# Context transposes by the PSUM bank, a bank for each value block, and the second layer's tables ahead of its weights

## The chip, the cores and the metric

The kernel runs on one core of one Trainium2 chip. Time is the device time of that core in microseconds, from the first to the last instruction of one execution. It was 2702.51 us before the change, the median of three runs (2702.22 to 2703.63).

## What is computed

Two layers over 512 latent tokens and 256 context tokens, 1024 channels each, in float32. Cut to what matters here:

```python
for l in range(2):
    h_lat = rmsnorm(x, g_norm1[l]) * (1 + sc1) + sh1          # 512 tokens
    h_ctx = rmsnorm(ctx, g_norm1[l]) * (1 + csc1) + csh1      # 256 tokens
    p_lat = h_lat @ w_in[l]       # queries, keys, values, two convolutions, gates
    p_ctx = h_ctx @ w_in[l]       # in the last layer keys and values alone
    q, k  = rope(rmsnorm(heads(...)))        # per head; the context's without rope
    x   = x + gt1 * (merge of attention and convolutions) @ w_o[l]
    x   = x + gt2 * relu(modulated norm of x @ w_mlp_in[l])**2 @ w_mlp_out[l]
    # ctx goes the same way in the first layer
return rmsnorm(x, g_final)
```

Latent queries attend to latent and context keys together, context queries to context keys alone.

## The kernel before

**Numbers.** Every float32 operand of a matmul is split into a high and a low half, and one product is three matmuls (`mm3`: L163 high by high, L164 high by low, L165 low by high). Weights come by SP's DMA queue into a ring of four raw buffers `wraw` (L126 for query and key columns, L128 for others); ACT casts the high half (L134, `whi`), and DVE or POOL subtracts for the low one (L136, `wlo`).

**Tiles.** Tokens stand in six blocks of 128, four latent and two of context (in the trace of the second layer's start these are the last two that the first layer's MLP makes). Activations go into the matmuls transposed, channels on partitions, in eight tiles (`k` or `j` from 0 to 7, called columns below). PSUM has two pools that matter: `pa` tiles of two banks, `pb` tiles of one bank.

**From the residual stream to a projection** (`modulate`). When a block's MLP output is complete in PSUM, DVE multiplies it by the gate (L1116, `gt`) and adds it to the residual (L1117), ACT sums its squares (L1093), POOL makes the root (L378, L379), DVE scales the block (L1095). Then PE transposes column by column (L428). For the 512 latent tokens one column fills a bank, for the 256 context tokens half of one. Each column is evicted twice: ACT writes the high half (L433, modulated by scale and shift), and a second copy is made from the same PSUM, by DVE for even columns (L438) and by ACT for odd ones (L436); DVE subtracts for the low half (L439). Before the change the two columns of a context bank are transposed one after the other, each in its own step.

**Queries, keys, values.** The combined projection of queries and keys runs for the latent tokens, then for context. Four `pb` tiles are copied out by ACT (L500) and DVE (L502), squared on ACT (L512), turned by the rotary tables on DVE (L522, L525; the tables are multiplied by the gains at L472), scaled on POOL (L555, L563, L565) and transposed (L534). The values (`v_heads`) take two token blocks into the two halves of one `pb` tile, and each half is split on its own (ACT L156, DVE L159). Scores, softmax and the products with the values follow (L665 to L693).

**What sets the order.** The code is a set of generators that are stepped beside one another; a scheduler then fixes the order of the instructions of each engine, by its own estimate of times, and that order is the program. `next_in` is the step that puts the second layer's first loads, table products, modulation and projection beside the end of the first layer's MLP. `tc.issue_after(x)` keeps an instruction behind `x`. Each engine works through its own list in order, and SP's list is that of the loads.

## Time and profile before

| | |
|---|---|
| median of three runs | 2702.51 us |
| the profiled execution's own time | 2700.5 us |
| its span | 2698.7 us |
| granted TensorE clock, mean | 0.999 |
| PE busy | 2672.6 us (99%) |
| DVE / ACT / POOL busy | 1624.6 / 873.9 / 693.3 us |

Spans and shares are those of one execution. A row of a timeline gives start, duration, engine, line, operation, names out<-in, sizes, and in brackets the idle time of the engine ahead of it with what ended it. Matmuls overlap: the distance from one start to the next is what one costs, 0.23 us for 512 columns, while the duration of one is longer. A wait of PE is counted only where PE itself was idle.

### The profile page before, as it was taken

What the parts mean: (1) busy time and instruction counts of PE and PEld (TensorE: products, weight loads), DVE (VectorE), ACT (ScalarE), POOL (GpSimd) and SP (SyncE); (2) the same over time, 40 slices, a digit from 0 to 9 for tenths busy, and PEclk for the clock granted to TensorE, in tenths of its full rate; (3) what the DMA queues carried; (4) which work ended last, traced back from release to release, by engine and by line L of the source; (5) the groups of instructions that cost most, each with busy time, mean ns of one, the idle gap of its engine ahead of it and who ended that gap; (6) DMA issues with size and microseconds to landing.
All of it is one profiled execution on the core that took longest, in us unless ns stands there. A gap on an engine that the chain in (4) does not pass through costs nothing.

```text
span 2698.7 us, 36188 instructions
## 1 busy us (share of the span) xinstructions
PE 2672.6 (99%) x14571; PEld 2300.5 (85%) x14571; DVE 1624.6 (60%) x2098; ACT 873.9 (32%) x1426; POOL 693.3 (26%) x593
## 2 busy tenths in 40 slices
PE   8999999999999999999999999999999999999998
PEld 5899888888888888888888888998888888888887
DVE  5656837897764335585445356657578645644545
ACT  4556222122212323412121235563223233422223
POOL 1433432243221220201010103335445212111102
PEclk9999999999999999999999999999999999999999
DMA  7211324432275243344334232114333634432332
GB/s 255 64 35 58 98 77 141 133 107 66 82 228 157 63 144 94 97 159 153 110 104 146 79 110 87 55 60 122 120 114 102 181 112 144 132 95 94 110 101 94
DMA packets 341983, 302.50 MB, mean 112 GB/s; under 512 B 10577, under 2 KB 288385, under 8 KB 341817
## 3 DMA queue, kind: packets, MB, share of 16 engines
q1 hardware_dynamic: 340400, 298.81, 35.8%
q8 instruction: 114, 1.87, 0.3%
q10 hardware_dynamic: 1416, 1.39, 0.2%
q14 instruction: 53, 0.43, 0.0%
HBM read 274.96 MB, written 25.20 MB: 111 GB/s over the span
## 4 chain that ended last, share of the span: by engine, by line
PE 96%; DVE 2%; DMA 1%; ACT 1%; issue 0%; POOL 0%; SPq 0%; POOLq 0%; ACTq 0%; DVEq 0%
PE pa L163 21%; PE pa L165 21%; PE pa L164 21%; PE pb L163 9%; PE pb L165 8%; PE pb L164 8%; PE pb L676 2%; PE pb L690 1%; PE pb L693 1%; PE pb L691 1%; DVE tx L522 1%; PE pa L428 0%; DVE wlo L136 0%; PE pb L918 0%; PE pb L784 0%
## 5 line engine op out<-in xcount | busy, mean ns | idle before, releaser
L163 PE MATMUL pa<-ta,whi 128*128 128x512 f32 (+1 forms) x2896 | 1023.9, 354 | 0.0
L164 PE MATMUL pa<-ta,wlo 128*128 128x512 f32 (+1 forms) x2896 | 1020.1, 352 | 0.0
L165 PE MATMUL pa<-ta,whi 128*128 128x512 f32 (+1 forms) x2896 | 1019.6, 352 | 0.0
L134 ACT CAST whi<-wraw 128x1024 fp32r<-128x1024 f32 x360 | 377.8, 1051 | 1036.5 <-PE pa L165 404.3
L163 PEld LDWEIGHTS pa<-ta,whi 128*128 128x128 f32 x2896 | 547.9, 189 | 78.5 <-issue 2.5
L165 PEld LDWEIGHTS pa<-ta,whi 128*128 128x128 f32 x2896 | 547.4, 189 | 75.0 <-DVE ta L439 0.2
L164 PEld LDWEIGHTS pa<-ta,wlo 128*128 128x128 f32 x2896 | 548.0, 189 | 73.4
L163 PE MATMUL pb<-whi,ta 128*128 128x512 f32 (+1 forms) x1200 | 435.2, 363 | 3.5 <-ACT ta L433 1.9
L165 PE MATMUL pb<-wlo,ta 128*128 128x512 f32 (+1 forms) x1200 | 432.5, 361 | 1.5 <-DVE wlo L136 1.5
L164 PE MATMUL pb<-whi,ta 128*128 128x512 f32 (+1 forms) x1200 | 432.9, 361 | 0.0
L760 DVE SCALAR_TENSOR_TENSOR pv<-tx,cols,pv 128x783 f32<-128x783 f32 (+1 forms) x448 | 400.9, 895 | 12.6
L136 DVE TENSOR_TENSOR wlo<-wraw,whi 128x1024 fp32r<-128x1024 f32 x248 | 322.7, 1304 | 89.3 <-ACT whi L134 83.5
L136 POOL TENSOR_TENSOR wlo<-wraw,whi 128x1024 fp32r<-128x1024 f32 x112 | 270.2, 2414 | 360.2 <-ACT whi L134 308.0
L163 PEld LDWEIGHTS pb<-whi,ta 128*128 128x128 f32 x1200 | 226.8, 189 | 41.7 <-ACT ta L433 2.6
L982 POOL TENSOR_TENSOR ta<-ta 128x768 fp32r<-128x768 f32 (+1 forms) x64 | 105.0, 1641 | 600.2 <-DVE ta L981 593.7
L165 PEld LDWEIGHTS pb<-wlo,ta 128*128 128x128 f32 x1200 | 226.7, 189 | 35.2 <-DVE wlo L136 1.7
L164 PEld LDWEIGHTS pb<-whi,ta 128*128 128x128 f32 x1200 | 227.0, 189 | 34.7 <-issue 0.8
L315 DVE SCALAR_TENSOR_TENSOR tx<-wraw,cs,tx 128x1024 f32<-128x1024 f32 x112 | 157.9, 1424 | 49.0 <-DMA wraw<-in_w_mod 44.1
L979 DVE TENSOR_SCALAR ta<-pa 128x512 f32<-128x512 f32 (+1 forms) x63 | 51.8, 822 | 192.5 <-PE pa L165 181.9
L1116 DVE TENSOR_TENSOR ta<-pb,gt 128x512 f32<-128x512 f32 x100 | 68.8, 688 | 160.0 <-PE pb L165 159.9
L803 ACT ACTIVATE ta<-pa 128x768 f32<-128x768 f32 (+1 forms) x52 | 36.6, 705 | 223.8 <-PE pa L165 215.1
L159 POOL TENSOR_TENSOR ta<-tx,ta 128x768 fp32r<-128x768 f32 (+1 forms) x32 | 52.6, 1643 | 156.2 <-ACT ta L156 151.7
(188 smaller groups left out, 2352.0 us busy)
## 6 DMA issues: line engine op xcount, KB each, us to landing
wraw<-in_w_in SPq DMA_DIRECT2D x144, 512.0 KB
wraw<-in_w_mod SPq DMA_DIRECT2D x80, 512.0 KB
wraw<-in_w_mlp_out SPq DMA_DIRECT2D x72, 512.0 KB
wraw<-in_w_mlp_in SPq DMA_DIRECT2D x64, 512.0 KB
wraw<-in_w_o SPq DMA_DIRECT2D x24, 512.0 KB
tx<-spill SPq DMA_DIRECT2D x24, 384.0 KB
ta<-in_w_mod SPq DMA_DIRECT2D x32, 256.0 KB
wraw<-in_w_attn_out SPq DMA_DIRECT2D x16, 512.0 KB
```

What stands on the lines that cost most here:

```text
L134: nc.scalar.copy(hi, raw)
L136: self.last_lo = self.lo_engine.tensor_tensor(lo, raw, hi.bitcast(F32), op=ALU.subtract)
L159: (eng or nc.gpsimd).tensor_tensor(lo, src, hi.bitcast(F32), op=ALU.subtract)
L163: nc.tensor.matmul(ps, ah, bh, start=start, stop=False)
L164: nc.tensor.matmul(ps, al, bh, start=False, stop=False)
L165: self.last_pe = nc.tensor.matmul(ps, ah, bl, start=False, stop=stop)
L315: nc.vector.scalar_tensor_tensor(acc[b], raw, c, acc[b], op0=ALU.mult, op1=ALU.add)
L676: nc.tensor.transpose(pt[:, b * 256 + q * P:b * 256 + (q + 1) * P], probs[n, part][q][:, o], self.ident)
L760: nc.vector.scalar_tensor_tensor((v if t == K_CF - 1 else pv)[:, 0:n], u[:, t:t + n], c["cf"](t, k), (v if t == 1 else pv)[:, 0:n], op0=AL ...
L979: nc.vector.tensor_scalar(out=v[:, 0:n], in0=ps[:, 0:n], scalar1=0.0, scalar2=None, op0=ALU.max)
L982: nc.gpsimd.tensor_tensor(lo[:, 0:n], v[:, 0:n], hi[:, 0:n].bitcast(F32), op=ALU.subtract)
L1116: nc.vector.tensor_tensor(t, ps, gt[:, o], op=ALU.mult)
```

## The change

Five things are done.
- `modulate`: for a wide tile with context tokens, both columns of a bank are transposed in the even column's step, four transposes in a row.
- `v_heads`: each of the six value blocks has a `pb` tile of its own. The weights of the values are requested ahead of the late keys (`w_v`).
- Keys and queries: in the first layer the context's pair, in the second layer the second latent pair too, are made after these requests (`late`).
- `next_in`: the rotary tables of the second layer are requested first, its query and key weights behind the last of them; the products of tables and gains move from ahead of the projection to its middle (`CTX_FROM` is 4).
- Gate rows and the last norm's gains are requested behind the last weight load so far. In `scores`, the context's two matmul groups run one behind the other before the first softmax.

```diff
--- before.py
+++ after.py
@@ -123,9 +123,9 @@
         raw = self.W("wraw", N_RAW, shape)
         if isinstance(src, list):
             for k, part in enumerate(src):
-                nc.sync.dma_start(out=raw[:, k].rearrange("p (s c) -> p s c", s=2), in_=part)
+                self.last_load = nc.sync.dma_start(out=raw[:, k].rearrange("p (s c) -> p s c", s=2), in_=part)
         else:
-            nc.sync.dma_start(out=raw, in_=src)
+            self.last_load = nc.sync.dma_start(out=raw, in_=src)
         return raw
 
     def halves(self, raw, shape):
@@ -366,7 +366,8 @@
         got = []
         for b in range(nb):
             t = self.small.tile([P, D], F32, name="gt", tag="gt", bufs=2)
-            self.nc.sync.dma_start(out=t, in_=self.gates[l, r][b:b + 1, :].broadcast_to([P, D]))
+            with self.tc.issue_after(self.last_load.ins):
+                self.nc.sync.dma_start(out=t, in_=self.gates[l, r][b:b + 1, :].broadcast_to([P, D]))
             got.append(t)
         return got
 
@@ -420,12 +421,17 @@
             if wide and not pre and j % (1024 // n) == 0:
                 pa = self.PA()
             at = j % (1024 // n) * n
+            bank = 512 // n if wide else 1
             if pre:
                 ps = pre.pop(0)
             else:
+
                 ps = pa[:, at:at + n] if wide else self.PB()
-                for q, xn in enumerate(xns):
-                    nc.tensor.transpose(ps[:, q * P:(q + 1) * P], xn[:, j * P:(j + 1) * P], self.ident)
+                to = pa[:, at:] if wide else ps
+                for u in range(bank if j % bank == 0 else 0):
+                    for q, xn in enumerate(xns):
+                        nc.tensor.transpose(to[:, u * n + q * P:u * n + (q + 1) * P],
+                                            xn[:, (j + u) * P:(j + u + 1) * P], self.ident)
             a = self.scale[l][:, which, b, j:j + 1]
             s0 = 0 if which == 0 else 24
             sh = self.mc[l][:, b, s0 + j:s0 + j + 1]
@@ -461,7 +467,7 @@
             gains.append(g)
         for g in gains:
             rope = self.X(D)
-            nc.sync.dma_start(out=rope, in_=i["rope"])
+            self.last_rope = nc.sync.dma_start(out=rope, in_=i["rope"])
             ropes.append(rope)
         self.tables = gains, ropes
 
@@ -576,7 +582,9 @@
         kt = self.new_pairs(2)
         new_queries(0)
         gains, ropes = self.tables
-        for p, (tk, tq) in enumerate(pairs):
+        pairs = list(enumerate(pairs))
+        late = pairs[2 if l == 0 else 1:]
+        for p, (tk, tq) in pairs[:len(pairs) - len(late)]:
             key(tk, p)
             query(0, tq, p)
         pa = self.PA()
@@ -588,22 +596,23 @@
                 c = slice((NB_L + b) * P, (NB_L + b + 1) * P)
                 self.mm3(ps[b][:, o], hs[k][0][:, c], hs[k][1][:, c], ws[k][0][:, o], ws[k][1][:, o],
                          k == 0, k == KT - 1)
-        tk, tq = self.qk_out(ps, full)
-        key(tk, 2)
-        if full:
-            query(0, tq, 2)
+        late.append((2, self.qk_out(ps, full)))
+        w_v = self.w_rows(w, 0, OFF_V, 256)
+        for p, (tk, tq) in late:
+            key(tk, p)
+            if tq is not None:
+                query(0, tq, p)
         vt = self.new_pairs(2)
 
         def v_heads():
-            ws = self.w_rows(w, 0, OFF_V, 256)
+            ws = w_v
             for p in range(3):
-                ps = self.PB()
                 for b in range(2):
-                    blk = 2 * p + b
-                    self.gemm_tm(ps[:, b * 256:(b + 1) * 256], ws, hs, blk)
+                    blk, ps = 2 * p + b, self.PB()
+                    self.gemm_tm(ps[:, 0:256], ws, hs, blk)
                     hi, lo = vt[blk // 3]
                     o = slice((blk % 3) * 256, (blk % 3 + 1) * 256)
-                    self.split(ps[:, b * 256:(b + 1) * 256], hi[:, o], lo[:, o], eng=nc.vector)
+                    self.split(ps[:, 0:256], hi[:, o], lo[:, o], eng=nc.vector)
                 yield True
 
         spill = [self.spill([P, T]) for _ in range(8)]
@@ -648,7 +657,9 @@
                     p = self.A() if part else self.X(T)
                 else:
                     sv = s[:, q * TC:(q + 1) * TC]
-                    self.mm3(sv, qh[:, o], ql[:, o], kh[:, TL:T], kl[:, TL:T], True, True)
+                    for u in range(2 if q == 0 else 0):
+                        c = slice((blk + u) * P, (blk + u + 1) * P)
+                        self.mm3(s[:, u * TC:(u + 1) * TC], qh[:, c], ql[:, c], kh[:, TL:T], kl[:, TL:T], True, True)
                     p = self.X(TC)
                 a = 4 * q
                 nc.vector.tensor_reduce(out=m[:, a:a + 1], in_=sv, axis=AX.X, op=ALU.max)
@@ -1017,7 +1028,8 @@
             self.bg.append(nxt)
         else:
             gf = self.small.tile([P, D], F32, name="gt", tag="gt", bufs=2)
-            nc.sync.dma_start(out=gf, in_=i["g_final"][None, :].broadcast_to([P, D]))
+            with self.tc.issue_after(self.last_load.ins):
+                nc.sync.dma_start(out=gf, in_=i["g_final"][None, :].broadcast_to([P, D]))
             self.g_final = gf
             self.ys = {}
         self.lo_engine = nc.vector
@@ -1213,15 +1225,18 @@
     def next_in(self, ws):
 
         l = DEPTH - 1
-        raws = [self.w_qk(self.i["w_in"][l], u) for u in range(KT // 2)]
         self.rotary_in(l)
+        with self.tc.issue_after(self.last_rope.ins):
+            raws = [self.w_qk(self.i["w_in"][l], u) for u in range(KT // 2)]
         for raw in raws:
             ws += self.qk_halves(raw)
-        self.rotary()
         ctx = self.ctx_in(l)
         for k in range(KT):
             for _ in range(4 if k == 0 else 1):
                 next(self.lat, None)
+            if k == CTX_FROM:
+                with self.tc.issue_after(self.last_dve.ins):
+                    self.rotary()
             for _ in range(CTX_STEP if k >= CTX_FROM else 0):
                 next(ctx, None)
             yield True
```

Line numbers shift: after the change the transposes are L433 (before L428), ACT's evictions L439 and L442 (L433, L436), DVE's L444 and L445 (L438, L439), the copies L506 and L508 (L500, L502), the rotary products L528 and L531 (L522, L525), the tables' product L478 (L472), and the residual chain L1105, L1107, L1128, L1129 (L1093, L1095, L1116, L1117).

Three places of the new order. The first is PE at the start of the second layer. Before, the end of the MLP's last block, four latent transposes (column 6), and the projection:

```order
L164 MATMUL pb<-whi,ta 128x512
L165 MATMUL pb<-wlo,ta 128x512
L428 MATMUL pa<-ident,tx 128x128 [waits PE_49,Activation_49]
L428 MATMUL pa<-ident,tx 128x128 x3
L163 MATMUL pb<-whi,ta 128x512 [waits Activation_49]
L164 MATMUL pb<-whi,ta 128x512
L165 MATMUL pb<-wlo,ta 128x512 [waits DVE_49]
L163 MATMUL pb<-whi,ta 128x512
```

After, from the latent columns 6 and 7 on, with the context's twelve transposes behind them:

```order
L433 MATMUL pa<-ident,tx 128x128 [waits PE_49,Activation_49]
L433 MATMUL pa<-ident,tx 128x128 x3
L433 MATMUL pa<-ident,tx 128x128 [waits DVE_49]
L433 MATMUL pa<-ident,tx 128x128 x3
L433 MATMUL pa<-ident,tx 128x128 [waits PE_49,Activation_49]
L433 MATMUL pa<-ident,tx 128x128 [waits DVE_49]
L433 MATMUL pa<-ident,tx 128x128 x2
L433 MATMUL pa<-ident,tx 128x128 [waits PE_49,Activation_49]
L433 MATMUL pa<-ident,tx 128x128 x3
L433 MATMUL pa<-ident,tx 128x128 [waits DVE_49,Activation_49]
L433 MATMUL pa<-ident,tx 128x128 x3
L163 MATMUL pb<-whi,ta 128x512 [waits Activation_49]
```

Twenty transposes stand together now. In the order, the wait for DVE ahead of the context's second transpose is for the last context block's norm (L1107), the last wait for DVE and ACT is for both evictions of the first context bank, and the matmul's wait is for the cast of its weights on ACT.

The second is ACT at the same place, with `pa_13757` and `pa_13811` (before) and `pa_13814` (after) latent tiles, `pa_13930` and `pa_13979` context tiles. Before, the cast `whi_13861` of the projection's first weights and what follows it:

```order
L134 CAST whi_13861<-wraw_13841 128x1024 [waits DMAHW5_49,DMAHW4_49,PE_49]
L433 ACTIVATE ta_13609<-pa_13757,mc1_149,scale1_151 128x512 [waits DVE_49,PE_49]
L436 ACTIVATE ta_13771<-pa_13757,mc1_149,scale1_151 128x512
L134 CAST whi_13865<-wraw_13844 128x1024 [waits DMAHW7_49,DMAHW6_49,PE_49]
L134 CAST whi_13869<-wraw_13847 128x1024 [waits DMAHW1_49,DMAHW0_49,PE_49]
L134 CAST whi_13873<-wraw_13850 128x1024 [waits DMAHW3_49,DMAHW2_49,PE_49]
L433 ACTIVATE ta_13611<-pa_13811,mc1_149,scale1_151 128x512 [waits PE_49]
L1093 ACTIVATE pa_13829,st_13830<-tx_9676 128x1024 [waits DVE_49,Activation_49]
```

After, from the squares of the last context block to the first of these casts, `whi_13864`:

```order
L1105 ACTIVATE pa_13832,st_13833<-tx_9679 128x1024 [waits DVE_49,Activation_49]
L439 ACTIVATE ta_13616<-pa_13814,mc1_149,scale1_151 128x512 [waits DVE_49,PE_49]
L442 ACTIVATE ta_13828<-pa_13814,mc1_149,scale1_151 128x512
L439 ACTIVATE ta_13602<-pa_13930,mc1_149,scale1_151 128x256 [waits PE_49]
L439 ACTIVATE ta_13610<-pa_13979,mc1_149,scale1_151 128x256 [waits PE_49]
L439 ACTIVATE ta_13604<-pa_13930,mc1_149,scale1_151 128x256 [waits DVE_49]
L442 ACTIVATE ta_13940<-pa_13930,mc1_149,scale1_151 128x256
L439 ACTIVATE ta_13606<-pa_13930,mc1_149,scale1_151 128x256 [waits PE_49]
L439 ACTIVATE ta_13608<-pa_13930,mc1_149,scale1_151 128x256 [waits DVE_49]
L442 ACTIVATE ta_13964<-pa_13930,mc1_149,scale1_151 128x256
L134 CAST whi_13864<-wraw_13852 128x1024 [waits DMAHW6_49,DMAHW5_49]
```

The first cast moved from ahead of the last context block's squares to behind the evictions of context columns 0 to 4.

The third is DVE in the first layer, where `pa_590` holds context columns 0 to 3 and `ta_720` (after: `ta_722`) is the copy of column 2. Before, from the last copy of the projection's results on:

```order
L502 COPY tx_640<-pb_304 128x256 [waits Activation_49]
L522 TENSOR_TENSOR tx_660<-tx_633,tx_438 128x512 [waits DVE_49]
L438 TENSOR_SCALAR ta_720<-pa_590,scale0_150,mc0_148 128x256 [waits Activation_49]
L522 TENSOR_TENSOR tx_654<-tx_633,tx_438 128x512 [waits Activation_49]
L522 TENSOR_TENSOR tx_678<-tx_634,tx_440 128x512 [waits DVE_49]
```

After:

```order
L508 COPY tx_640<-pb_304 128x256 [waits Activation_49]
L528 TENSOR_TENSOR tx_660<-tx_633,tx_438 128x512 [waits DVE_49]
L528 TENSOR_TENSOR tx_654<-tx_633,tx_438 128x512 [waits Activation_49]
L528 TENSOR_TENSOR tx_678<-tx_634,tx_440 128x512 [waits DVE_49]
L531 TENSOR_TENSOR tx_633<-tx_660,tx_654 128x512 [waits DVE_49]
L528 TENSOR_TENSOR tx_672<-tx_634,tx_440 128x512 [waits Activation_49]
L528 TENSOR_TENSOR tx_691<-tx_639,tx_438 128x512 [waits DVE_49]
L531 TENSOR_TENSOR tx_634<-tx_678,tx_672 128x512 [waits DVE_49]
L444 TENSOR_SCALAR ta_722<-pa_590,scale0_150,mc0_148 128x256 [waits PE_49]
```

The eviction moved from behind one rotary product to behind seven. On ACT, column 3's eviction stands behind sixteen squares there, and in the order the last four of these wait for the seventh product.

## Rows read from the trace of the kernel before

**Rows 1.** Page: busy us and share of engines; a group: busy, mean, idle time.

```profile
PE 2672.6 (99%) x14571; PEld 2300.5 (85%) x14571; DVE 1624.6 (60%) x2098; ACT 873.9 (32%) x1426; POOL 693.3 (26%) x593
...
L1116 DVE TENSOR_TENSOR ta<-pb,gt 128x512 f32<-128x512 f32 x100 | 68.8, 688 | 160.0 <-PE pb L165 159.9
```

**Rows 2.** Waits of PE over the span: us in total, times, longest us.

```profile
PE pa L428 <- DVE ta L438: 1.8, 2, 1.0
PE pb L690 <- DVE tx L159: 1.8, 2, 0.9
PE pb L165 <- DVE wlo L136: 1.5, 1, 1.5
PE pb L534 <- DVE ta L159: 1.1, 2, 0.6
PE pb L163 <- DVE ta L159: 0.9, 1, 0.9
```

**Rows 3.** Timeline of PE at the end of the MLP: start us, duration us.

```profile
1615.88 0.39 PE L165 MATMUL pb<-wlo,ta 128*128 128x512 f32 x1
...
1622.28 0.39 PE L165 MATMUL pb<-wlo,ta 128*128 128x512 f32 x1
1622.51 0.60 PE L428 MATMUL pa<-ident,tx 128*128 128x128 f32 x4
1622.86 0.48 PE L163 MATMUL pb<-whi,ta 128*128 128x512 f32 x1
```

**Rows 4.** Timeline of ACT, start of the second layer.

```profile
1618.88 1.03 ACT L134 CAST whi<-wraw 128x1024 fp32r<-128x1024 f32 x1
...
1639.91 0.56 ACT L433 ACTIVATE ta<-pa,mc,scale 128x256 fp32r<-128x256 f32 x1 [0.53 <-PE pa L428]
```

**Rows 5.** Timeline of DVE, start of the second layer.

```profile
1616.31 0.69 DVE L1116 TENSOR_TENSOR ta<-pb,gt 128x512 f32<-128x512 f32 x1
1617.03 0.69 DVE L1117 TENSOR_TENSOR tx<-tx,ta 128x512 f32<-128x512 f32 x1
...
1619.92 0.75 DVE L1095 TENSOR_SCALAR tx<-tx,st 128x1024 f32<-128x1024 f32 x1 [0.74 <-POOL st L379]
...
1625.19 0.69 DVE L1117 TENSOR_TENSOR tx<-tx,ta 128x512 f32<-128x512 f32 x1
...
1629.06 0.75 DVE L1095 TENSOR_SCALAR tx<-tx,st 128x1024 f32<-128x1024 f32 x1 [0.72 <-POOL st L379]
...
1640.52 0.54 DVE L438 TENSOR_SCALAR ta<-pa,scale,mc 128x256 f32<-128x256 f32 x1 [0.67 <-ACT ta L433]
```

**Rows 6.** Window: length, busy us by engine, then PEclk (granted clock), DMA.

```profile
24.00:28.00 4.00, 2.34 (x8) 1.47 (x7) 2.46 (x8) 2.85 (x4) 0.00 (x0) 0.72 1.10 348
```

**Rows 7.** Timeline of PE at the start of the kernel.

```profile
23.70 0.66 PE L274 MATMUL pa<-ident,ta 128*128 128x128 f32 x4 [1.38 <-DVE ta L271]
26.01 0.79 PE L163 MATMUL pb<-whi,ta 128*128 128x512 f32 x1 [1.66 <-ACT ta L433]
...
29.81 0.40 PE L163 MATMUL pb<-whi,ta 128*128 128x512 f32 x1
```

**Rows 8.** Timeline of PE in the first layer, its waits of 64 to 71 us.

```profile
64.39 0.44 PE L428 MATMUL pa<-ident,tx 128*128 128x128 f32 x2 [0.88 <-ACT ta L436]
65.32 0.39 PE L163 MATMUL pb<-whi,ta 128*128 128x256 f32 x1 [0.50 <-ACT whi L134]
...
69.62 0.44 PE L428 MATMUL pa<-ident,tx 128*128 128x128 f32 x2 [0.80 <-DVE ta L438]
70.56 0.50 PE L164 MATMUL pa<-whi,ta 128*128 128x512 f32 x1 [0.49 <-DVE ta L439]
```

**Rows 9.** Timeline of DVE in the first layer.

```profile
61.29 0.68 DVE L522 TENSOR_TENSOR tx<-tx 128x512 f32<-128x512 f32 x1
61.89 0.54 DVE L438 TENSOR_SCALAR ta<-pa,scale,mc 128x256 f32<-128x256 f32 x1
```

**Rows 10.** Timeline of ACT in the first layer: one of the squares.

```profile
60.84 0.31 ACT L512 ACTIVATE tx<-tx 128x128 f32<-128x128 f32 x1
```

## Prediction, made before the changed kernel was run

> **What bounds the kernel now.** I read the page's busy times first. PE is busy 99% of the span, 2672.6 of 2698.7 us, and no other engine passes 60% [rows 1]. So an edit off PE pays only where PE waits for it, and all that can be won is PE's idle time, 26 us. PE's waits, the second view, say whom it waited for [rows 2]: the eviction of context transposes (L428, from DVE 1.8 us), the weights of the values (L165, 1.5), the shared bank of two value blocks (L163 for L159, 0.9), the keys' transposes and the context scores (L534 1.1, L690 1.8). Third, the timelines of the two places where the edits sit: 62 to 71 us (first layer, context norm beside the queries and keys) and 1616 to 1660 us (start of the second layer). The reader should see that at the second place PE does not wait at all: the MLP's last matmul is issued at 1622.28, four transposes follow at 1622.51, and the second layer's projection starts at 1622.86 [rows 3]. It can, since ACT cast its first weights at 1618.88, before the MLP had ended [rows 4].
>
> **The change, part by part, in the numbers of the profiled run** (2700.5 us with a span of 2698.7; the median of three runs is 2702.5, 2.0 above it, and I carry the difference to the median).
>
> *Second layer, the new order.* This is the large term. After the change PE has twenty transposes in a row behind the MLP, twelve of them the context's, and only then the first projection matmul; that one waits for a cast which on ACT now stands behind the evictions of context columns 0 to 3. Those cannot start before the MLP has ended, since the last context block must first get its residual and its norm. What stands on PE while it waits is the whole projection; nothing can go past. The chain, from rows:
> - For the block before, the last matmul is issued at 1615.88 [rows 3], L1116 starts 0.43 us later, at 1616.31, and the normed block is there when L1095 ends, 1619.92 + 0.75 = 1620.67, 4.36 us behind that start [rows 5]. For the last block L1116 can start at about 1622.7, so its norm is ready at 1627.1. In the run shown the step from L1117 to L1095 took 3.87 us for that block and 2.89 for the one before, so 1628.1 is the late end.
> - Three further transposes and the way into PSUM: 0.5, so 1627.6.
> - First bank (columns 0, 1): ACT 0.56, then DVE 0.54, then ACT twice more, 0.56 each, with 0.05 where the engine changes [rows 4, 5]: 2.3, so 1629.9.
> - The second bank's transposes wait for both readers of the first bank: 0.55, so 1630.45. Its eviction takes 2.3 again up to the last ACT step, so 1632.75.
> - The cast, 1.03 [rows 4]: 1633.8.
>
> The projection thus starts 10.9 us later. Of this, 16 transposes at 0.11 us (0.35 for four [rows 3], and 0.09 on the matmul behind them) are work moved ahead, 1.8 us. PE idles **9.1 us** more, 10.1 at the late end. The three casts behind the first have 5.5 us of matmuls each as cover (24 at 0.23), so no second wait follows.
>
> *The clock behind that wait.* At the start of the kernel PE sat idle twice, for 1.4 and 1.7 us with four transposes between, and the granted clock of 24 to 28 us was 0.72 of full speed [rows 6], so the level of 1.2 GHz for part of it. Nine projection matmuls were issued between 26.01 and 29.81 [rows 7], 3.8 us, where 0.23 each (1622.28 to 1622.51 [rows 3]) makes 2.1. The new gap is longer, with few transposes in it, so I add these **1.7**; bounds 0 and 2.
>
> *What goes in the second layer.* Transposes stood inside the projection and one pair waited 1.0 us (the longest of L428's two [rows 2]); in the new order that wait is gone: **-1.0**. The weights of the values are requested, cast and split before the late keys: the 1.5 at L165 goes, but DVE now splits weights ahead of the second pair's products, so the keys come later and some of it returns at their transposes. I take **-1.0**, between -1.5 and 0.
>
> *The tables.* Loaded first, they end DVE's idle time before L472. PE did not wait for it, and in the new order the two products stand between evictions, where 0.6 us of ACT work covers half of each; the rest lies in the late end above. The weight loads now behind the tables on SP wait for buffers that DVE frees in any case, and their casts come 14 us later than before: nothing. If that cover were gone, the loss would be the landing of two loads behind a queue, some 2 us.
>
> *First layer, whole banks.* In 64 to 71 us PE waited four times, 0.88, 0.50, 0.80 and 0.49 us, together 2.7 [rows 8], and a bank at once looks like the cure. But DVE and ACT are full there. DVE evicted column 2 at 61.89, behind one product of the rotary step [rows 9]; now seven products stand ahead of it, 0.60 us each from 61.29 on, so it ends at 66.0. ACT's eviction of column 3 stands behind squares that need the seventh product, done at 65.5; four of them take 1.2 us [rows 10], two evictions 1.0, and it ends at 67.7. On PE, the cast that it waited for until 65.32 has these two evictions no longer ahead of it: 64.3, where PE is ready at 63.5 (64.39 less 0.88): a wait of 0.8. Eight value matmuls of half the width follow, 1.0 in all, to 65.3, and then four transposes that wait for column 3: 2.4. A further 0.4 follows at the first matmul that needs the low half, which DVE makes late. That is 3.6 against 2.7. I take **0**, between -2.7 (all four waits gone) and +1.2.
>
> *Value blocks, a bank each.* The row shows PE held 0.9 us by the eviction of the other half of its bank [rows 2]; four banks let it go on: **-0.9**.
>
> The Trainium skill, page "PSUM — Partial Sum Buffer", section "PSUM bank collisions raise a hardware error", says that access of two engines to one bank has to be kept apart by bank, two readers included. That favours a bank for each value block, and speaks against a bank shared by ACT's and DVE's halves. The trace agrees: DVE's L438 starts at 1640.52, 0.05 us after ACT's read of the same bank ended, and its row names ACT as what ended its idle time [rows 4, 5]. With readers side by side the chain above would be some 1.0 us shorter and the sum +6.9.
>
> *Gates.* Requested later on SP. The group that uses them sat idle 160.0 us, of which PE ended 159.9 [rows 1], and in the new order the loads still stand ahead of most weights of the gemm whose result they scale: nothing. Without that cover, a landing of some 2 us. *Context scores* (both matmul groups first): same matmuls, same waits for the softmax: 0, give or take 0.5.
>
> **Sum:** 9.1 + 1.7 - 1.0 - 1.0 - 0.9 = **+7.9 us**, 2708.4 for a run like the profiled one, **2710.4** on the scale of the median. What measurements of this kernel can tell from no change is 0.2%, 5.4 us.
>
> **Rivals.**
> - *The waits it aims at go.* All four of 64 to 71 us (-2.7), the whole 1.5 (-0.5 more), and the later waits at L534 and L690 ease as ACT, DVE and POOL get ahead during PE's new wait (up to -2.9 [rows 2]). That gives +1.8, or 2704.3, no change by the measure; with the clock kept it would be 2702.6. For it: DVE's and ACT's work there is no more than before. Against: their order puts the evictions later. Chance 0.22.
> - *Faster: the first cast is not held back.* It needs two loads only, which have long landed. Should ACT be free for it at about 1622, the wait of 9.1 and the clock's 1.7 fall away, and what is left is the gains: -2.7 - 1.0 - 1.5 - 0.9 = -6.1, or 2696. It decides whether the first projection matmul comes within 2 us of the MLP's end. Against: ACT works through its list in order, and before the cast in it stand evictions that need the last block's norm. Chance 0.05.
> - *Worse.* The late end of the chain (+1.0), the late keys giving back the whole 1.0, and the first layer at +1.2: +11.1, or 2713.6. For it: DVE is full where the keys are made. Chance 0.15.
>
> My forecast holds 0.58. The range, 2703 to 2714.5, takes in the worse case and most of the no-change case. Below it lies some 0.1 (the faster case and the lowest of no change), above it 0.05. Slower by over 0.2% (2707.9 or more): 0.73, the forecast and the worse case; within: 0.22; faster: 0.05.
>
> **What would show it.** The chain holds if PE's waits list a new one of the projection's L163 for ACT's cast, with the transposes' waits beside it some 9 us of idle between 1622 and 1634, and the granted clock is below 1 in the stretch behind. The first layer is as I say if PE's idle time of 60 to 72 us is 2.7 us or more, with one wait of over 2 us for ACT. The value terms hold if L163 no longer waits for L159 nor L165 for L136. I am wrong if the projection starts within 3 us of the MLP's end, or if the first layer loses its waits altogether.

## The result, and the profile of the changed kernel

The change made the kernel **slower: 2716.25 us** (median of five runs, 2715.02 to 2719.77) against 2702.51 (five runs, 2702.12 to 2703.63), a ratio of 1.0051 with a 95% interval of 1.0040 to 1.0062. That is +13.7 us where +7.9 was forecast, and 1.75 us above the range. The profiled execution took 2717.89 us with a span of 2716.1; its busy times answer to [rows 1].

Page of after, busy us, share and instructions of each engine:

```profile
PE 2679.7 (99%) x14571; PEld 2306.3 (85%) x14571; DVE 1629.2 (60%) x2098; ACT 873.7 (32%) x1426; POOL 683.2 (25%) x593
```

PE has the same 14571 instructions and is busy 7.1 us longer: matmuls that ran slower. The other 10.3 of the span's 17.4 are idle time. Its waits answer to [rows 2] (us in total, times, longest):

```profile
PE pb L163 <- ACT whi L134: 4.0, 2, 3.2
PE pa L433 <- ACT ta L442: 3.8, 2, 2.3
...
PE pb L540 <- DVE st L666: 1.7, 2, 1.2
PE pa L163 <- DVE tx L809: 1.4, 1, 1.4
...
PE pb L701 <- DVE st L669: 1.3, 2, 0.6
```

New are the projection's wait for a cast, 3.2 us, the transposes' waits, two at the late keys (L540 for L666), two of the context products (L701) and one at L809. L163 for L159 and L165 for L136 are gone, as forecast.

**Start of the second layer.** Timeline of PE in after, from the last MLP matmul (start, duration, in brackets the idle time ahead and what ended it); [rows 3] had 0.58 us there:

```profile
1630.47 0.39 PE L165 MATMUL pb<-wlo,ta 128*128 128x512 f32 x1
1630.70 0.60 PE L433 MATMUL pa<-ident,tx 128*128 128x128 f32 x4
1633.10 0.85 PE L433 MATMUL pa<-ident,tx 128*128 128x128 f32 x5 [1.80 <-DVE ta L444]
1635.31 1.76 PE L433 MATMUL pa<-ident,tx 128*128 128x128 f32 x7 [1.37 <-DVE tx L1107]
1638.63 1.11 PE L433 MATMUL pa<-ident,tx 128*128 128x128 f32 x4 [1.56 <-ACT ta L442]
1642.97 0.79 PE L163 MATMUL pb<-whi,ta 128*128 128x512 f32 x1 [3.22 <-ACT whi L134]
...
1648.13 0.40 PE L163 MATMUL pb<-whi,ta 128*128 128x512 f32 x1
```

The projection starts 12.5 us behind the MLP. The twelve matmuls from 1642.97 to 1648.13 then took 5.16 us, where 0.23 each makes 2.76. The granted clock says why (windows: length, busy us of PE, PEld, DVE, ACT, POOL, then PEclk, DMA share, GB/s):

```profile
1630.00:1634.00 4.00, 2.15 (x13) 1.43 (x11) 2.80 (x4) 2.13 (x4) 0.27 (x2) 1.00 0.00 0
1634.00:1638.00 4.00, 1.76 (x7) 1.36 (x7) 2.56 (x5) 2.70 (x5) 0.47 (x1) 0.54 0.00 0
1638.00:1642.00 4.00, 1.11 (x4) 0.71 (x4) 2.94 (x5) 2.18 (x6) 0.00 (x0) 0.50 0.02 4
1642.00:1646.00 4.00, 3.03 (x7) 2.46 (x8) 3.90 (x8) 3.69 (x5) 0.00 (x0) 0.50 0.09 20
1646.00:1650.00 4.00, 4.00 (x15) 3.12 (x15) 2.58 (x3) 1.07 (x2) 0.00 (x0) 0.75 0.87 268
```

From about 1634 PE ran at 1.2 GHz, through the context's transposes too, and came back to 2.4 only 5 us after the projection had begun. The DMA share is 0.00 up to 1638 and 0.02 up to 1642, so it was no load that held the cast: on ACT it follows the last of the evictions ahead of it without idle time. DVE, then ACT, in the same stretch:

```profile
1630.90 0.69 DVE L1128 TENSOR_TENSOR ta<-pb,gt 128x512 f32<-128x512 f32 x1 [1.26 <-PE pb L165]
...
1634.51 0.75 DVE L1107 TENSOR_SCALAR tx<-tx,st 128x1024 f32<-128x1024 f32 x1 [0.74 <-POOL st L380]
...
1640.39 0.54 DVE L444 TENSOR_SCALAR ta<-pa,scale,mc 128x256 f32<-128x256 f32 x1 [1.06 <-ACT ta L439]
```

```profile
1636.26 0.56 ACT L439 ACTIVATE ta<-pa,mc,scale 128x256 fp32r<-128x256 f32 x1 [1.01 <-PE pa L433]
...
1638.02 0.56 ACT L442 ACTIVATE ta<-pa,mc,scale 128x256 f32<-128x256 f32 x1
1639.79 0.56 ACT L439 ACTIVATE ta<-pa,mc,scale 128x256 fp32r<-128x256 f32 x1 [1.21 <-PE pa L433]
1640.96 0.56 ACT L439 ACTIVATE ta<-pa,mc,scale 128x256 fp32r<-128x256 f32 x1 [0.61 <-DVE ta L444]
1641.43 0.56 ACT L442 ACTIVATE ta<-pa,mc,scale 128x256 f32<-128x256 f32 x1
1641.88 1.04 ACT L134 CAST whi<-wraw 128x1024 fp32r<-128x1024 f32 x1
```

**First layer.** Timeline of PE in after, the stretch of [rows 8]:

```profile
65.47 0.38 PE L163 MATMUL pb<-whi,ta 128*128 128x256 f32 x1 [0.79 <-ACT whi L134]
...
68.94 1.12 PE L433 MATMUL pa<-ident,tx 128*128 128x128 f32 x4 [2.26 <-ACT ta L442]
70.14 0.80 PE L164 MATMUL pa<-whi,ta 128*128 128x512 f32 x1
...
74.14 0.53 PE L164 MATMUL pa<-whi,ta 128*128 128x512 f32 x1
```

The waits are those worked out beforehand, 0.8 and 2.3. What was not foreseen stands behind them: nine matmuls in the 4.00 us from 70.14 to 74.14, where 0.23 each makes 2.1. The windows of after and, under them, of before:

```profile
64.00:68.00 4.00, 1.90 (x12) 1.23 (x10) 4.00 (x8) 3.89 (x22) 3.83 (x5) 0.95 0.00 0
68.00:72.00 4.00, 2.98 (x8) 2.21 (x9) 4.00 (x8) 1.85 (x4) 3.83 (x5) 0.50 0.00 0
72.00:76.00 4.00, 4.00 (x16) 3.25 (x15) 1.57 (x4) 1.91 (x4) 3.14 (x7) 0.70 0.46 131
```

```profile
64.00:68.00 4.00, 3.12 (x15) 2.44 (x16) 4.00 (x9) 4.00 (x19) 4.00 (x1) 1.00 0.00 0
68.00:72.00 4.00, 2.71 (x14) 1.78 (x13) 3.98 (x7) 2.49 (x5) 3.92 (x2) 1.00 0.00 0
```

Four waits of up to 0.88 us, with matmuls between them, had left the clock at 1.00; 0.79 and 2.26, with eight short matmuls between them, did not.

**Where the time went.** PE does the same work in both kernels, so the start of a matmul can be compared with that of the one at the same place in the work (the same sum of columns done). How far after is behind the profile of before, worked out from the two timelines, with a second profile of after (e11 below) beside it:

| at (us, before) | after | again | step | what lies in the step |
|---|---|---|---|---|
| 53 | +1.2 | -0.1 | | loads at the start; differs between executions |
| 79 | +3.7 | +1.9 | +2.4 / +2.0 | whole banks, with the clock behind them |
| 88 | +2.5 | +0.7 | -1.2 / -1.2 | value blocks |
| 220 | +5.7 | +4.0 | +3.2 / +3.3 | context scores |
| 569 | +8.3 | +6.7 | +2.6 / +2.7 | waits at 558 and 567 |
| 1660 | +17.1 | +15.6 | +8.8 / +8.9 | start of the second layer |
| 1701 | +17.6 | +16.1 | +0.5 / +0.5 | late keys |

### The profile page after: what moved, and what is told of

It is laid out like the page before. It is cut to its first block, busy times and chain, and to the rows that moved or that the text cites. A ratio compares the mean times of both kernels' runs of the same rounds, so it can differ in the third digit from the quotient of the medians.

```text
span 2716.1 us, 36174 instructions
## 1 busy us (share of the span) xinstructions
PE 2679.7 (99%) x14571; PEld 2306.3 (85%) x14571; DVE 1629.2 (60%) x2098; ACT 873.7 (32%) x1426; POOL 683.2 (25%) x593
## 4 chain that ended last, share of the span: by engine, by line
PE 89%; DVE 1%; ACT 0%; issue 0%; POOL 0%; POOLq 0%; ACTq 0%; DVEq 0%
PE pa L163 21%; PE pa L164 20%; PE pa L165 20%; PE pb L163 8%; PE pb L164 8%; PE pb L165 8%; PE pb L687 1%; PE pb L701 1%; PE pb L704 1%; PE pb L702 1%; PE pa L433 0%; PE pb L929 0%; PE pb L795 0%; PE pb L327 0%; DVE pv L771 0%
## 5 line engine op out<-in xcount | busy, mean ns | idle before, releaser
L163 PE MATMUL pa<-ta,whi 128*128 128x512 f32 (+1 forms) x2896 | 1024.6, 354 | 2.0 <-DVE tx L809 1.4
L165 PE MATMUL pa<-ta,whi 128*128 128x512 f32 (+1 forms) x2896 | 1020.3, 352 | 0.0
L163 PEld LDWEIGHTS pa<-ta,whi 128*128 128x128 f32 x2896 | 548.2, 189 | 81.1 <-issue 3.3
L165 PEld LDWEIGHTS pa<-ta,whi 128*128 128x128 f32 x2896 | 547.7, 189 | 74.6 <-DVE ta L445 0.2
L163 PE MATMUL pb<-whi,ta 128*128 128x512 f32 (+1 forms) x1200 | 435.3, 363 | 5.9 <-ACT whi L134 4.0
L165 PE MATMUL pb<-wlo,ta 128*128 128x512 f32 (+1 forms) x1200 | 432.6, 361 | 0.0
L136 DVE TENSOR_TENSOR wlo<-wraw,whi 128x1024 fp32r<-128x1024 f32 x248 | 322.9, 1305 | 92.0 <-ACT whi L134 86.2
L136 POOL TENSOR_TENSOR wlo<-wraw,whi 128x1024 fp32r<-128x1024 f32 x112 | 268.9, 2403 | 363.6 <-ACT whi L134 311.4
L163 PEld LDWEIGHTS pb<-whi,ta 128*128 128x128 f32 x1200 | 227.5, 190 | 43.9 <-ACT whi L134 5.7
L165 PEld LDWEIGHTS pb<-wlo,ta 128*128 128x128 f32 x1200 | 227.4, 190 | 34.0
L993 POOL TENSOR_TENSOR ta<-ta 128x768 fp32r<-128x768 f32 (+1 forms) x64 | 104.8, 1638 | 600.3 <-DVE ta L992 593.8
L1128 DVE TENSOR_TENSOR ta<-pb,gt 128x512 f32<-128x512 f32 x100 | 68.8, 688 | 161.9 <-PE pb L165 161.8
L159 POOL TENSOR_TENSOR ta<-tx,ta 128x768 fp32r<-128x768 f32 (+1 forms) x32 | 52.5, 1641 | 156.4 <-ACT ta L156 152.0
```

What stands on the lines that cost most here:

```text
L136: self.last_lo = self.lo_engine.tensor_tensor(lo, raw, hi.bitcast(F32), op=ALU.subtract)
L159: (eng or nc.gpsimd).tensor_tensor(lo, src, hi.bitcast(F32), op=ALU.subtract)
L163: nc.tensor.matmul(ps, ah, bh, start=start, stop=False)
L165: self.last_pe = nc.tensor.matmul(ps, ah, bl, start=False, stop=stop)
L993: nc.gpsimd.tensor_tensor(lo[:, 0:n], v[:, 0:n], hi[:, 0:n].bitcast(F32), op=ALU.subtract)
L1128: nc.vector.tensor_tensor(t, ps, gt[:, o], op=ALU.mult)
```

## The experiments

Each was timed beside the kernel before on its own chip; "before" is that median.

**e1: only the guard on the loads taken from after.** In `next_in`:

```diff
-        with self.tc.issue_after(self.last_rope.ins):
-            raws = [self.w_qk(self.i["w_in"][l], u) for u in range(KT // 2)]
+        raws = [self.w_qk(self.i["w_in"][l], u) for u in range(KT // 2)]
```

> The changed kernel without one line: the second layer's query and key weights are no longer held behind the last rotary table on SP. In its order the first cast then stands on ACT ahead of the last context block's squares, and four transposes instead of twenty stand ahead of the projection; nothing else on PE moves. Theory 1 (the guard made the scheduler put cast and projection late, and PE idles for that): PE's waits of 1630 to 1643 us go, no wait of L163 for L134 over 1 us there, granted clock 1.00 behind the MLP, and 11 to 12 us less than the changed kernel: 2704 to 2706 us. Rival (the twelve context transposes by the bank, or the tables' late loads, hold PE at this place): the projection still starts 4 us or more behind the MLP's end, and the time stays above 2710 us.

Measured 2707.17 us (before 2702.98; ratio 1.0015, 1.0006 to 1.0023). PE in e1, at the start of the second layer:

```profile
1630.49 0.39 PE L165 MATMUL pb<-wlo,ta 128*128 128x512 f32 x1
1630.72 0.60 PE L433 MATMUL pa<-ident,tx 128*128 128x128 f32 x4
1631.07 0.47 PE L163 MATMUL pb<-whi,ta 128*128 128x512 f32 x1
```

The projection follows the MLP again. One line on the loads' order costs 13.7 - 4.2 = 9.5 us, and its own place is where it shows: counted as in the table, e1 and after are 8.2 behind alike at 1620 us and 10.7 apart at 1660. The time is 1.2 above the range of theory 1 and well below that of the rival.

**e2: the same part alone**, put into before: tables first, guard, products in the middle.

```diff
-        raws = [self.w_qk(self.i["w_in"][l], u) for u in range(KT // 2)]
         self.rotary_in(l)
+        with self.tc.issue_after(self.last_rope.ins):
+            raws = [self.w_qk(self.i["w_in"][l], u) for u in range(KT // 2)]
...
-        self.rotary()
...
+            if k == CTX_FROM:
+                with self.tc.issue_after(self.last_dve.ins):
+                    self.rotary()
```

> The kernel before with one part alone: the second layer's tables requested first with the guard on its weights, and the table products in the middle of the projection. No whole banks, no own value banks, no change of the first layer. Theory 1: the wall comes with this part alone, eighteen transposes ahead of the projection and the first cast behind the context evictions; 11 to 13 us above the kernel before, less 1.0 for the transposes' wait that goes: 2712 to 2715 us. Rival (it takes whole banks as well): within 3 us of the kernel before, at most 2705.5 us.

Measured 2712.93 us (ratio 1.0040, 1.0028 to 1.0053), +10; in its trace the start of the second layer takes 11.0. The wait needs nothing else of the change.

**e3: whole banks alone** (`modulate` as changed, all else as before).

```diff
...
+                for u in range(bank if j % bank == 0 else 0):
+                    for q, xn in enumerate(xns):
...
```

> The kernel before with whole banks of context transposes alone. In its order DVE's eviction of context column 2 in the first layer stands behind seven rotary products, as in the changed kernel, and the second layer starts as before. Theory 1 (the late evictions make up for the waits that go): PE's idle time of 60 to 72 us is 3 to 5 us, with one wait of over 2 us for ACT's eviction, and the time 2702.5 to 2705.5 us. Rival (whole banks cure the waits of 64 to 71 us, and the 3 us lost there in the changed kernel come from the value matmuls that moved in): idle there under 1.5 us and the time 2698.5 to 2701 us.

Measured 2705.97 us (ratio 1.0011, 1.0002 to 1.0020), +3.0; counted as in the table, 1.9 of it lies between 60 and 79 us. Timeline of PE, then the window behind:

```profile
68.08 1.12 PE L432 MATMUL pa<-ident,tx 128*128 128x128 f32 x4 [2.73 <-ACT ta L441]
69.28 0.80 PE L164 MATMUL pa<-whi,ta 128*128 128x512 f32 x1
```

```profile
68.00:72.00 4.00, 3.84 (x12) 2.94 (x13) 4.00 (x8) 1.61 (x4) 3.66 (x6) 0.58 0.00 0
```

The waits are 0.80 and 2.73, and the clock is down behind them without any other part of the change.

**e4: context scores alone.** Both context groups ahead of the first softmax:

```diff
-                    self.mm3(sv, qh[:, o], ql[:, o], kh[:, TL:T], kl[:, TL:T], True, True)
+                    for u in range(2 if q == 0 else 0):
+                        c = slice((blk + u) * P, (blk + u + 1) * P)
+                        self.mm3(s[:, u * TC:(u + 1) * TC], qh[:, c], ql[:, c], kh[:, TL:T], kl[:, TL:T], True, True)
```

> The kernel before with one part alone: both matmul groups of the context scores ahead of the first softmax, in the first layer. The changed kernel lost some 3 us between 120 and 220 us, with waits of 0.65 and 0.25 us at 168 and again at 215 us. Theory 1 (this part makes the context's products wait for a later softmax): the same waits, and 2704.5 to 2706 us. Rival (those waits come of the later keys or of the whole banks): no wait of over 0.3 us between 125 and 250 us, and within 0.8 us of the kernel before.

Measured 2705.34 us (ratio 1.0008, 0.9999 to 1.0017): +2.4, at the edge of what its interval tells from nothing. The trace is clearer: counted as in the table, e4 loses 3.2 between 88 and 220 us, as after does. PE has two new waits there, and two like them at 212 us, 1.8 us together. PE in e4, then DVE in e4, then DVE in before:

```profile
165.26 0.36 PE L692 MATMUL pb<-tx,ta 128*128 128x256 f32 x1 [0.64 <-DVE st L660]
...
166.91 0.63 PE L534 MATMUL pb<-ident,tx 128*128 128x128 f32 x4 [0.25 <-DVE tx L159]
```

```profile
161.76 1.29 DVE L522 TENSOR_TENSOR tx<-pb,tx 128x512 f32<-128x512 f32 x2 [4.63 <-ACT tx L512]
162.97 0.95 DVE L656 TENSOR_REDUCE st<-pa 128x1 f32<-128x768 f32 x1
163.83 0.68 DVE L525 TENSOR_TENSOR tx<-tx 128x512 f32<-128x512 f32 x1
164.43 0.68 DVE L159 TENSOR_TENSOR tx<-pb,tx 128x512 fp32r<-128x512 f32 x1
```

```profile
160.47 0.42 DVE L654 TENSOR_REDUCE st<-pb 128x1 f32<-128x256 f32 x1 [5.13 <-PE pb L165]
160.90 1.29 DVE L522 TENSOR_TENSOR tx<-pb,tx 128x512 f32<-128x512 f32 x2
...
162.22 0.69 DVE L525 TENSOR_TENSOR tx<-tx 128x512 f32<-128x512 f32 x1
162.83 0.68 DVE L159 TENSOR_TENSOR tx<-pb,tx 128x512 fp32r<-128x512 f32 x1
```

The split (L159) that the value products read starts 1.60 us later. L522, which waits for ACT's squares, starts 0.86 later, and a reduction of 768 elements now stands ahead of L525 and L159 on DVE, where in before one of 256 was done in DVE's idle time ahead of L522. Same matmuls, but another order on DVE. No run here parts the two halves of the 1.60, nor the 3.2 us into these waits and what lies beside them.

**e5: values alone** (`late`, `w_v` requested early, a `pb` tile for each block).

```diff
...
-        for p, (tk, tq) in enumerate(pairs):
...
+        late = pairs[2 if l == 0 else 1:]
...
+        w_v = self.w_rows(w, 0, OFF_V, 256)
...
-                ps = self.PB()
...
+                    blk, ps = 2 * p + b, self.PB()
...
```

> The kernel before with one part alone: a PSUM bank for each value block, the weights of the values requested ahead of the late keys, and the second layer's second key pair made late. Theory 1 (the two waits go, the late keys take some back): no wait of L163 for L159 at 84 us (-0.9 to -1.1), none of L165 for L136 in the second layer (-1.5), and 0 to 1 us more at the keys' transposes between 1670 and 1705 us: 1.5 to 2.6 us less than the kernel before, 2700.4 to 2701.5 against 2703.0. Rival (the late keys give the whole of it back): within 0.5 us of the kernel before, with over 2 us of waits at the keys' transposes there.

Measured 2700.74 us (before 2703.46; ratio 0.9992, 0.9983 to 1.0001), -2.7, just short of what its interval tells from nothing. The waits for L159 at 84 us and for L136 are gone, as in after.

**e6: gate loads alone** (`issue_after(self.last_load.ins)` around both).

```diff
...
+            with self.tc.issue_after(self.last_load.ins):
+                self.nc.sync.dma_start(out=t, in_=self.gates[l, r][b:b + 1, :].broadcast_to([P, D]))
...
```

> The kernel before with one part alone: gate rows and the last norm's gains requested behind the last weight load so far. Theory 1 (they stand ahead of most weights of the gemm that they scale): no wait of DVE's gate product for a load, within 0.8 us of the kernel before. Rival (a gate lands late, or the weights behind it do, and the changed kernel's 2 to 3 us at 560 to 575 us come of it): a wait of PE of over 1 us at 560 to 575 us or at the first gate products, and 1.5 us or more above the kernel before.

Measured 2703.06 us (before 2703.46; ratio 0.9998, 0.9989 to 1.0007): nothing.

**e7: e5, with the tables ahead of the last of the four weight loads instead of all four.**

```diff
-        raws = [self.w_qk(self.i["w_in"][l], u) for u in range(KT // 2)]
+        raws = [self.w_qk(self.i["w_in"][l], u) for u in range(3)]
         self.rotary_in(l)
+        with self.tc.issue_after(self.last_rope.ins):
+            raws += [self.w_qk(self.i["w_in"][l], u) for u in range(3, KT // 2)]
```

> The values' part alone, as in the run beside it, and the second layer's tables requested ahead of the last of its four query and key weights, the guard on that last one alone. In its order PE's and ACT's lists are those of the values' part; SP alone differs. Theory 1 (in the kernel before, DVE stood in its list at the table products, which waited for the tables, and the context's evictions behind them held PE for 1.0 us): the wait of L428 at 1636 us goes, DVE does not wait for the tables over 1 us, and 0.8 to 1.3 us less than the values' part alone. Rival (this wait comes of the evictions themselves): the wait stays and the two are within 0.4 us.

Measured 2699.34 us (ratio 0.9987, 0.9978 to 0.9995), the fastest here and below before. PE's one wait at the start of the second layer, 0.99 us in before (L428 for L438) and 2.55 in e5, is gone in e7. Its length varies where the tables come behind all the weights: 0.8 in e8, 1.3 in e4 and 1.5 in e6, with the order of before at this place. Its row in e5, and the window around it:

```profile
1639.41 0.44 PE L428 MATMUL pa<-ident,tx 128*128 128x128 f32 x2 [2.55 <-DVE ta L438]
```

```profile
1636.00:1640.00 4.00, 1.45 (x8) 0.93 (x7) 3.33 (x4) 0.11 (x1) 0.00 (x0) 1.00 0.03 12
```

The clock stayed at 1.00 there and in the window behind, although this wait is longer than the 2.26 us of after's first layer. PE did dense matmuls up to it and dense matmuls behind it.

So the tables can go ahead of a part of the weights without a new wait, if the first cast keeps its place. That e7 is 1.4 us below e5, beside the same runs of before, is within their two intervals.

**e8: the kernel before once more**, one execution.

> The kernel before once more, to see which of its waits come again. The changed kernel waits 1.4 and 0.6 us at 564 and 574 us for the merge's products on DVE; the kernel before did not in its profile. Theory 1 (that wait varies from run to run, since it also came, at 0.7 us, with the next layer's part alone, whose order is the same up to there): waits there between 0 and 2 us, and waits at 63 to 70, 84, 119, 1636 and 1658 us within 0.3 us of the first profile. Rival (it comes of the change): no wait there again.

Time 2701.56 us. The waits of [rows 8] came again, and two more:

```profile
558.76 0.50 PE L163 MATMUL pa<-ta,whi 128*128 128x512 f32 x1 [0.86 <-DVE tx L798]
567.95 0.47 PE L163 MATMUL pa<-ta,whi 128*128 128x512 f32 x1 [0.55 <-DVE ta L868]
```

The profile of before has neither. So of the 2.6 us that after lost near 558 us, 1.9 (counted as in the table) is lost by another execution of the unchanged kernel. That chance explains all of it isn't shown: the longer wait is 1.2 to 2.0 in the four profiles that have the values' and the gates' parts together (after twice, e1, e10) and 0 to 1.0 in the nine others. No run has these two parts alone.

**e9: e7 with one load less in front of the tables and both latent pairs early again** (against e7):

```diff
-        late = pairs[2 if l == 0 else 1:]
+        late = pairs[2:]
...
-        raws = [self.w_qk(self.i["w_in"][l], u) for u in range(3)]
+        raws = [self.w_qk(self.i["w_in"][l], u) for u in range(2)]
```

> The kernel before with the value changes and the second layer's tables requested ahead of the last two of its four weight loads, as in e7 but for one load more; and both latent pairs of keys and queries of the second layer are made ahead of the values' weights again (only the context's pair stays late). Theory 1 (the late pair of e5 and e7 costs what its waits show: L540 for L666 and L159 1.22 + 0.58 + 0.17 = 1.97 us in e5, against 0.78 + 0.85 = 1.63 before): a gain of 0.3 to 1 over e7, 2698.3 to 2699.2, the waits at the start of the scores of the second layer 1.6 or less. Rival (the late pair is the cover under which the values' weights are split): L165 waits for L136 again, 1.5, and the time is 2700.5 to 2701.5. A third outcome, that the tables one load earlier hold something back: a wait of over 2 us at the start of the second layer, 2701 to 2704.

Measured 2699.93 us (before 2702.89; ratio 0.9989, 0.9980 to 0.9998), no better than e7. The longest wait at the late keys stays at 1.2 (L534 for L658: 1.5 in two, as in e7), so that wait does not come from the pair being late, and L165 waits 0.36 for its weights again. Theory 1 falls, the rival holds in part. Another part is the clock. Behind the waits of 1.22 and 0.58 us at the scores, which e7 has too (1.21 and 0.58, clock at 1.00), it was down in e9:

```profile
1698.00:1702.00 4.00, 4.00 (x19) 3.60 (x18) 3.83 (x10) 2.73 (x7) 1.43 (x2) 0.58 0.46 135
```

Counted as in the table, that took 1.3 us.

**e10: after without whole banks and without the scores' new order** (both put back as in before; against after):

```diff
...
-                for u in range(bank if j % bank == 0 else 0):
-                    for q, xn in enumerate(xns):
...
+                    self.mm3(sv, qh[:, o], ql[:, o], kh[:, TL:T], kl[:, TL:T], True, True)
...
```

> The changed kernel with the whole banks and the context scores undone: the tables requested first with the weights behind them, the values and the gates as changed. Theory 1 (the first layer's terms add to the second layer's, which came out as forecast): 2716.25 less 3.0 (banks, from e3) less 2.4 (scores, from e4), so 2710 to 2711.5; by the forecast's own terms without the first layer's 2710.4. PE idles some 12 us between the last MLP matmul and the first projection matmul. Rival (part of the miss belongs to the second layer's new order, or to runs of the changed kernel being apart in other places): 2712.5 to 2716.

Measured 2712.03 us (before 2702.89; ratio 1.0037, 1.0025 to 1.0050), +9.1, between the two theories, 1.2 above the forecast's terms for these parts. In the first layer the value blocks' edits leave the waits at 0.88, 0.50, 0.33 and 0.49, and the clock at 1.00:

```profile
68.00:72.00 4.00, 3.18 (x18) 2.23 (x17) 4.00 (x8) 2.50 (x8) 3.92 (x2) 1.00 0.00 0
```

The 1.2 has a place in the trace. At 1711 us, behind waits of 1.22 and 0.58 us that after has too, the clock went down in e10 and not in after, which took 1.3 us (counted as in the table):

```profile
1712.00:1716.00 4.00, 4.00 (x25) 3.88 (x24) 2.76 (x7) 2.25 (x5) 0.91 (x1) 0.70 0.46 130
```

This profile is of the median run; the other four runs left no trace.

**e11: after once more**, one execution.

> The changed kernel once more, one look, to see which of its waits come again. Theory 1 (the order sets them): from the last MLP matmul to the first projection matmul 12.5 us (12.2 to 12.8), the waits of the scores 0.64 and 0.25 twice, those of 63 to 71 us 0.8, 2.3 and 0.5, the time 2715 to 2720. The waits near 558 us (1.4 and 0.6 in the first profile, 0.86 and 0.55 in a profile of the kernel before, none in its first) are expected anywhere from 0 to 2. Rival (the scores' waits or the banks' are chance): one of these is under 0.2 this time.

Time 2716.46 us. From the last MLP matmul to the projection 12.5 us, the scores' waits 0.64 and 0.26 twice, those of 63 to 70 us 0.79, 2.26 and 0.54: the order sets them. Near 558 us 1.50 and 0.57. The clock behind the first layer's waits was down for a shorter time than in after (windows of 66 to 70 and 70 to 74 us: 0.92 and 0.65, in after 0.70 and 0.50): the same waits, 2.0 us in the table instead of 2.4.

## Why the prediction was right in sign and wrong in size

Sign and largest cause were right, the size was not. Two steps failed, both in the first layer. Whole banks were put at 0 without a term for the clock behind a wait of over 2 us that the working itself had found, and took +2.4. Context scores were put at 0 because the matmuls and waits would stay the same, and took +3.2. Together that is 5.6 of the 5.8 us missed. The signs named beforehand came true (8.0 us of idle time where 9 was named), but none of them looked at the clock in the first layer or at the scores.

By its steps (measured: the steps of the table above, which without the start and the waits near 558 us make 2.4 - 1.2 + 3.2 + 8.8 + 0.5 = 13.7; that this is the difference of the medians is partly luck, since the waits near 558 us were longer in both profiles of after than in either of before):

- **Second layer's chain, +9.1.** The mechanism held link by link, though PE's idle time was 1.80 + 1.37 + 1.56 + 3.22 = 7.95 and not 9.1. L1128 came 0.43 us behind the MLP's last matmul (1630.47 to 1630.90), the norm ended 4.36 after that (1635.26; 4.36 was the forecast), and ACT's share of the first bank, 1636.26 to 1638.58, took the 2.3. Between these links two things were longer: ACT's first column came 1.0 us behind the norm (0.5 forecast), and the second bank came 1.2 us after the first was read (0.55). In both places transposes ran at 1.2 GHz: four took 1.11 where [rows 3] has 0.60. The projection starts 11.9 us later instead of 10.9, at the late end, though for another reason than the norm. Less the 1.8 of transposes moved ahead, that is +10.1.
- **Clock behind it, +1.7.** Twelve matmuls lost 5.16 - 2.76 = 2.4, above the upper bound of 2. The term belonged there, and it had to be charged to the transposes ahead as well.
- **Transposes' wait and values' weights, -1.0 and -1.0.** Counted as in the table, after catches up 1.15 us where before waits for L438, and 1.7 where before waits for L136, of which it gives 0.5 back at the late keys: -1.15 and -1.2. The second layer is +8.8, +9.3 with the late keys, and the forecast's four terms make +8.8. This is closer than the terms are: as measured they make 10.1 + 2.4 - 1.15 - 1.2 = 10.2, and the 0.9 between that and 9.3 is not explained here.
- **Value blocks, -0.9**: -1.2. A wait can cost more than its idle time: at 65.47 above, a wait of 0.79 stands in 1.18 us from one start to the next, where 0.23 is usual, 0.16 more.
- **First layer, whole banks, 0 between -2.7 and +1.2: mis-sized.** The idle time was worked out rightly (3.6 against 2.7; measured 0.79 + 2.26 + 0.54 = 3.6 in e11), and was then not taken: 0 was. And the clock was left out: one wait of over 2 us was forecast, the clock's price was charged to PE's waits in the second layer, and here it was not. The lower clock took 4.00 - 2.07 = 1.9. Alone (e3) the banks cost 3.0. The term would have needed bounds even so: the wait of 2.55 us in e5 cost no clock.
- **Context scores, 0 give or take 0.5: wrong**, +3.2 in the trace, +2.4 alone. "Same matmuls, same waits" looked at PE's work and not at DVE's order, where the reduction had moved.
- **Gates 0**: held (e6).

The rivals: that the waits of 64 to 71 us go did not happen; "faster" needed the cast at its old place, which is what e1 and e7 restore; "worse" came nearest, with the late end of the chain and part of the late keys right, but a first layer of only +1.2. The sentence on the PSUM bank held: in the new chain ACT's L439 starts at 1640.96, 0.03 us after DVE's read of the same bank ended (1640.39 + 0.54), and its row names DVE. The Trainium skill, page "PSUM — Partial Sum Buffer", section "PSUM bank collisions raise a hardware error", asks for that separation, and the trace agrees. In the order of the change that instruction waits for DVE, so no run here shows what two readers side by side would do.

What stays open: what sets the waits near 558 us, and what decides whether the clock goes down behind a given wait. Whole banks and scores cost 4.6 together (13.7 less e10's 9.1) and 5.4 as the sum of two runs; without e10's 1.3 us of lower clock at 1711 us the first figure would be 5.9, and the intervals allow all three.

## What to carry to other kernels

A load's place in its queue is also a place in the order of the engine that casts it: before putting anything ahead of weights, find the first instruction that needs them and what then stands in front of it. Give every wait that is longer than those the trace shows unharmed a term for the clock behind it, in each stage alike, with 0 as its lower bound: here it was 0 behind 2.55 us in e5, 1.3 behind 1.22 and 0.58 in e9 and e10, and 1.9 and 2.4 in after. In the first layer 2.7 us in four pieces cost no clock in before; 0.80 and then 2.73 in one piece did in e3. An edit that leaves the matmuls alone still has to be read on every other engine's list.

## What the runs showed of the hardware

- Four waits of 0.5 to 0.9 us (0.3 to 0.9 in e10) within 7 us left the granted clock at 1.00 in before and e10; 0.8 and then 2.26 or 2.73 us in the same place took it to 0.50 and 0.58 in the window behind (after, e3).
- The length of a wait alone does not tell: 2.55 us between dense matmuls left the clock at 1.00 (e5, 1636 to 1644 us), and waits of 1.2 and 0.58 us at the second layer's scores left it at 1.00 in after, e5 and e7 and took it down in e9 and e10.
- Where PE did only eleven transposes in 8 us (1634 to 1642 us of after), the clock was 0.54 and 0.50, and four of them took 1.11 us where 0.60 is usual.
- The clock came back late: PE had been issuing matmuls without a wait from 1642.97, and the level of 2.4 GHz returned at about 1648.
- The same program waits differently from one execution to the next in some places: near 558 us 0 and 0.86 us in two executions of before, 1.40 and 1.50 in two of after.
